# A state space mixer's output matmuls: the two halves of the groups in turn, state terms ahead of the local term

## The chip, the cores and the metric

The kernel runs on one core of one Trainium2 chip. Its time is the device time of one execution in microseconds (us). The kernel before ran three times, and one more execution was recorded by the hardware profiler. The engines are TensorE (PE, with its weight loads as PEld), VectorE (DVE), ScalarE (ACT), GpSimd (POOL) and SyncE (SP), which issues DMAs.

## The reference, cut to what matters

The network has four layers over 512 tokens of width 1024. The change lies in the mixer of the first one, a diagonal complex state space model with 64 groups of 16 channels and 64 states each:

```python
bu_re = jnp.einsum('bsgc,gpc->bsgp', u, bb_re)
bu_im = jnp.einsum('bsgc,gpc->bsgp', u, bb_im)
_, _, h_re, h_im = lax.associative_scan(
    _complex_linear_combine, (a_re_t, a_im_t, bu_re, bu_im), axis=1)
y = (jnp.einsum('bsgp,gcp->bsgc', h_re, c_re.astype(f32))
     - jnp.einsum('bsgp,gcp->bsgc', h_im, c_im.astype(f32)))
y = y + d_skip.astype(f32).reshape(N_GROUPS, SSM_GROUP) * u
y = jax.nn.gelu(y.reshape(bsz, seq, D_MODEL)).astype(x.dtype)
val, gate = jnp.split(y @ w_glu, 2, axis=-1)
return (val * jax.nn.sigmoid(gate)) @ w_out
```

After it come a layer norm, a feed-forward layer, an attention layer with its own feed-forward layer, and two more layers of another kind.

## The kernel before, in words

The mixer (`s5`) cuts the 512 tokens into 64 chunks of 8. Within a chunk the output is a sum of two terms. The local term is the chunk's own input times a block Toeplitz matrix `T` (contraction over all 128 partitions, 8 tokens by 16 channels). The state term is the state at the chunk's start, `H`, times an output matrix `ca`, with a real and an imaginary part (`r` = 0, 1; contraction over 64 states).

The 64 groups are taken as two halves `h` of 32. The half `h` = 0 has its states on partitions 0 to 63, and its 64 chunks fill output partitions 0 to 63; the half `h` = 1 has the other 64 of both. The 32 groups of a half are taken in four rounds `q` of eight (`j`). For each round there are these steps:

- `state_in(q)` builds input matrices with PE (L692) and multiplies the input by them (L700), into two PSUM banks `e`. L700 takes `h` = 0 and `h` = 1 in turn.
- `states(q)` scans the 64 chunks on DVE (L109, L724) and leaves `H`. The scan's input and `H` are tiles with the tag `gi`, which has three buffers.
- `outmat(q)` computes `ca` on DVE. For rounds 0 and 1 it lies in the memory that the GLU's input `yl` takes over later (tag `xl`).
- `local(q)` computes the Toeplitz matrix's coefficients with PE (L760, in four strips of 32 columns), adds the skip term on DVE (`ks`, L119) and writes them to DRAM (`kd`, L766). `toeplitz(q)` reads them back as `T` with eight DMAs (L775). There are two `T` buffers.
- `outputs(q)` multiplies both terms into four PSUM banks, one for each `h` and each `jj` (four of the eight `j`), and applies the GELU (L793, ACT). L789 is the local term, L791 the state term. An fp32 matmul stands in the trace as two records.
- `place(q)` transposes the result on PE (L127) and splits it into a rounded part and a rest (`xh` on ACT, `xl` on DVE).

`head_a`, `head_b` and `head_c` are the first matmuls of the GLU behind it (L265 to L267), interleaved with the last rounds. The steps are called in the order 'outputs(0), states(2), outmat(3), local(2), toeplitz(2), outputs(1), place(0), local(3), toeplitz(3), states(3), place(1), outputs(2), place(2), head_a, outputs(3), head_b, place(3), head_c'. A planner then orders the instructions of each engine: it simulates the program and takes, among the instructions that are ready, the one that stands first in the program. Each engine works through its list in that order. Two matmuls that write the same PSUM bank keep their order.

Of the kernel before, what the change touches and what calls it, by code (L numbers as in the profile page):

```python
# [16 lines left out]
P = 128  # L17
# [49 lines left out]
class Net:  # L67
# [428 lines left out]
    def s5(self, x, lam_re, lam_im, log_dt, b_re, b_im, c_re, c_im, d_skip, early=None, w_glu=None):  # L496
        nc = self.nc
# [5 lines left out]
        with self.tc.tile_pool(name="s5b", bufs=1, side="right", reuse_waits="tile") as pb, \  # L503
# [11 lines left out]
            if early:  # L515
                p, w = early
# [127 lines left out]
            for r in range(2):  # L644
                G.memset(bz[r], 0.0)
                for h in range(2):
                    sl = slice(h * 64, h * 64 + 64)
# [6 lines left out]
            u = self.tile(pb, [P, 32, P], F32, "u")  # L654
# [124 lines left out]
            def outputs(q):  # L779
                ca, H, T = (st[q][k] for k in ("ca", "H", "T"))  # L780
                yg = st[q]["yg"] = self.tile(pb, [P, 8, 8, 16], F32, "yg", 2)
                for jj in range(2):
                    pss = [self.bank(), self.bank()]
                    for h in range(2):
                        sl = slice(h * 64, h * 64 + 64)
                        for m in range(4):
                            j = jj * 4 + m
                            o = pss[h][sl, m * P:(m + 1) * P]
                            nc.tensor.matmul(o, u[:, q * 8 + j, sl], T[:, m * 2 + h, jj], start=True, stop=False)  # L789
                            for r in range(2):  # L790
                                nc.tensor.matmul(o, H[sl, r, j], ca[sl, r, j].rearrange("p d c -> p (d c)"),  # L791
                                                 start=False, stop=r == 1)
                        nc.scalar.activation(yg[sl, :, jj * 4:jj * 4 + 4].rearrange("p t j c -> p j t c"),  # L793
                                             pss[h][sl].rearrange("p (j t c) -> p j t c", j=4, t=8),
                                             AF.Gelu_apprx_tanh)
# [68 lines left out]
            state_in(3)  # L864
            head_load(0)
            outputs(0)
            states(2)
            outmat(3, V)
            local(2)
            toeplitz(2)  # L870
            outputs(1)
            yh, yl = self.fm_x()
            place(0)
            local(3)
            toeplitz(3)
            states(3)
            place(1)
            outputs(2)
            place(2)
            head_a(0)  # L880
# [905 lines left out]
```

## Time and profile before

| | |
|---|---|
| median of three runs | 2530.16 us (2527.28 to 2530.75) |
| profiled execution | 2529.88 us, span 2528.1 us |
| mean granted TensorE clock | 0.973 of full speed |
| PE busy | 2411.3 us, 95% |
| DVE, ACT, POOL busy | 1559.1, 968.8, 389.0 us |

The span runs from the first to the last instruction. Records name the line of the kernel, the output and inputs by the program's names (buffer numbers left out), and the shape. In a timeline the first column is the start, the second the length of the merged piece, and in brackets stands the idle time of the engine before it and what ended it. A PE record lasts until its result is out, so records overlap: the rate is read from starts. The granted clock is given as a share of 2.4 GHz.

### The profile page before, as it was taken

The numbers are of one execution on the slowest core, as the hardware profiler recorded it, in microseconds if no ns is written. First come the engines' busy times: TensorE is split into PE (matmuls) and PEld (weight loads), VectorE is DVE, ScalarE is ACT, GpSimd is POOL, SyncE is SP. The second block draws the span as 40 slices with busy tenths as digits, with TensorE's granted clock in tenths as the row PEclk, the third lists the DMA queues.
The fourth block names the chain that finished last, engine by engine and source line by source line (L and its number), as shares of the span: only waits on it lengthen the run. The fifth ranks groups of instructions, "written<-read, shape, count | busy, mean of one in ns | idle before, by whom it ended". The sixth has DMA issues, their size and how long they took to land.

```text
span 2528.1 us, 30717 instructions
## 1 busy us (share of the span) xinstructions
PE 2411.3 (95%) x11961; PEld 1988.5 (79%) x11961; DVE 1559.1 (62%) x2898; ACT 968.8 (38%) x1563; POOL 389.0 (15%) x378
## 2 busy tenths in 40 slices
PE   7799999999989999999999999999989998999997
PEld 6667888888877888888776878888877687888886
DVE  8744366765666567765695573555569556355655
ACT  4213235445245335444246432333324643223331
POOL 1100110000231220000246220000034622000001
PEclk9779999999999999999999999999999999999999
DMA  4224243322221533222232235232123123423211
GB/s 110 57 57 133 84 150 101 98 88 81 85 71 51 167 92 109 92 92 67 78 127 51 84 121 179 67 133 67 60 86 127 51 86 107 167 67 117 84 59 59
DMA packets 182897, 237.55 MB, mean 94 GB/s; under 512 B 19728, under 2 KB 118816, under 8 KB 182688
## 3 DMA queue, kind: packets, MB, share of 16 engines
q1 hardware_dynamic: 182752, 235.59, 29.5%
q8 instruction: 94, 1.54, 0.3%
q14 instruction: 51, 0.42, 0.1%
HBM read 224.56 MB, written 11.01 MB: 93 GB/s over the span
## 4 chain that ended last, share of the span: by engine, by line
PE 82%; DVE 15%; ACT 2%; DMA 1%; issue 1%; SPq 0%; DVEq 0%; POOL 0%; ACTq 0%
PE ps L265 26%; PE ps L266 25%; PE ps L267 25%; PE ps L127 3%; DVE x L119 2%; PE ps L791 2%; DVE sc L1451 2%; DVE m L1450 2%; DVE x L109 1%; PE ps L789 1%; PE ps L459 1%; DVE vy L109 1%; DVE xl L109 1%; DVE ab L109 1%; DVE sc L119 1%
## 5 line engine op out<-in xcount | busy, mean ns | idle before, releaser
L109 POOL TENSOR_TENSOR wl<-wr,wh 128x1024 fp32r<-128x1024 f32 (+4 forms) x124 | 278.2, 2253 | 1810.9 <-ACT wh L249 1127.0
L249 ACT CAST wh<-wr 128x1024 fp32r<-128x1024 f32 (+4 forms) x300 | 305.7, 1021 | 578.8 <-PE ps L266 287.4
L267 PE MATMUL ps<-xh,wl 128*128 128x512 f32 x1248 | 485.9, 390 | 4.3 <-DVE wl L109 4.3
L265 PE MATMUL ps<-xh,wh 128*128 128x512 f32 x1248 | 486.2, 390 | 0.0
L266 PE MATMUL ps<-xl,wh 128*128 128x512 f32 x1248 | 486.2, 390 | 0.0
L109 DVE TENSOR_TENSOR wl<-wr,wh 128x1024 fp32r<-128x1024 f32 x176 | 217.2, 1236 | 226.5 <-ACT wh L249 225.4
L109 DVE TENSOR_TENSOR wl<-wq,wh 128x1024 fp32r<-128x1024 f32 x140 | 170.5, 1221 | 178.1 <-ACT wh L249 177.7
L267 PEld LDWEIGHTS ps<-xh,wl 128*128 128x128 f32 x1248 | 234.7, 188 | 53.4 <-DVE wl L109 4.7
L265 PE MATMUL ps<-wh,xh 128*128 128x512 f32 (+4 forms) x704 | 270.9, 386 | 4.5 <-DVE rp L109 2.0
L266 PEld LDWEIGHTS ps<-xl,wh 128*128 128x128 f32 x1248 | 234.8, 188 | 48.8
L265 PEld LDWEIGHTS ps<-xh,wh 128*128 128x128 f32 x1248 | 234.6, 188 | 48.6
L266 PE MATMUL ps<-wl,xh 128*128 128x512 f32 (+4 forms) x704 | 263.6, 375 | 0.0
L267 PE MATMUL ps<-wh,xl 128*128 128x512 f32 (+4 forms) x704 | 262.6, 376 | 0.5 <-DVE xl L109 0.5
L249 ACT CAST wh<-wq 128x1024 fp32r<-128x1024 f32 x140 | 147.3, 1052 | 284.1 <-PE ps L266 234.5
L266 PE MATMUL ps<-wl,sh 128*128 128x512 f32 x560 | 217.8, 389 | 0.0
L267 PE MATMUL ps<-wh,sl 128*128 128x512 f32 x560 | 217.5, 389 | 0.0
L265 PE MATMUL ps<-wh,sh 128*128 128x512 f32 x560 | 216.9, 389 | 0.0
L265 PEld LDWEIGHTS ps<-wh,xh 128*128 128x128 f32 x704 | 136.9, 195 | 31.4 <-ACT xh L122 3.5
L267 PEld LDWEIGHTS ps<-wh,xl 128*128 128x128 f32 x704 | 136.1, 194 | 22.1 <-DVE xl L109 1.1
L266 PEld LDWEIGHTS ps<-wl,xh 128*128 128x128 f32 x704 | 137.0, 195 | 18.5
L109 DVE TENSOR_TENSOR x<-x,ps 128x512 f32<-128x512 f32 x156 | 103.0, 681 | 73.4 <-PE ps L267 73.1
L127 PE MATMUL ps<-ident,x 128*128 128x128 f32 x576 | 97.6, 289 | 47.3 <-DVE x L119 30.8
(368 smaller groups left out, 3910.8 us busy)
## 6 DMA issues: line engine op xcount, KB each, us to landing
wr<-in_w_ffn_in_dram SPq DMA_DIRECT2D x44, 1024.0 KB, 5.1
wr<-in_w_ff_dram SPq DMA_DIRECT2D x40, 1024.0 KB, 5.5
wq<-in_w_ff_dram SPq DMA_DIRECT2D x24, 1024.0 KB, 5.1
wq<-in_w_ffn_out_dram SPq DMA_DIRECT2D x16, 1024.0 KB, 8.2
wr<-in_w_in_dram SPq DMA_DIRECT2D x12, 1024.0 KB, 5.5
wr<-in_w_ple_gate_dram SPq DMA_DIRECT2D x8, 1024.0 KB, 5.1
wr<-in_ssm_w_glu_dram SPq DMA_DIRECT2D x6, 1024.0 KB, 5.6
xs<-x SPq DMA_DIRECT2D x24, 256.0 KB, 2.0
```

What stands on the lines that cost most here:

```text
L109: (eng or self.nc.vector).tensor_tensor(out, a, b, op)
L119: (eng or self.nc.vector).scalar_tensor_tensor(out, a, s, b, op0, op1)
L127: self.nc.tensor.transpose(out, in_, self.ident[:k, :k])
L249: self.nc.scalar.copy(hi, src)
L265: mm(ps, lh, rh, start=first, stop=False)
L266: mm(ps, lh, rl, start=False, stop=False)
L267: mm(ps, ll, rh, start=False, stop=last)
L459: self.nc.tensor.matmul(bk[:, c], w[:, kt], self.Xh(kt)[:, c], start=kt == 0 and w is hi, stop=False)
L789: nc.tensor.matmul(o, u[:, q * 8 + j, sl], T[:, m * 2 + h, jj], start=True, stop=False)
L791: nc.tensor.matmul(o, H[sl, r, j], ca[sl, r, j].rearrange("p d c -> p (d c)"), start=False, stop=r == 1)
L1450: self.nc.vector.max(m8, s)
L1451: self.nc.vector.match_replace(s, m8, s, -3e38)
```

## The change

In `outputs`, the loop over the two halves goes inside the loop over `m`. For each `m` the four state matmuls come first: the real part of half 0 and half 1, then the imaginary part of half 0 and half 1. Then come the two local matmuls, half 0 and half 1. The first state matmul now clears the bank region (`start`), and the local one ends the accumulation (`stop`). The two GELUs come after all matmuls of a `jj`. Operands, banks and the number of instructions stay the same.

```diff
-                    for h in range(2):
-                        sl = slice(h * 64, h * 64 + 64)
-                        for m in range(4):
-                            j = jj * 4 + m
-                            o = pss[h][sl, m * P:(m + 1) * P]
-                            nc.tensor.matmul(o, u[:, q * 8 + j, sl], T[:, m * 2 + h, jj], start=True, stop=False)
-                            for r in range(2):
-                                nc.tensor.matmul(o, H[sl, r, j], ca[sl, r, j].rearrange("p d c -> p (d c)"),
-                                                 start=False, stop=r == 1)
+                    halves = [slice(h * 64, h * 64 + 64) for h in range(2)]
+                    for m in range(4):
+                        j = jj * 4 + m
+                        o = [pss[h][sl, m * P:(m + 1) * P] for h, sl in enumerate(halves)]
+                        for r in range(2):
+                            for h, sl in enumerate(halves):
+                                nc.tensor.matmul(o[h], H[sl, r, j], ca[sl, r, j].rearrange("p d c -> p (d c)"),
+                                                 start=r == 0, stop=False)
+                        for h, sl in enumerate(halves):
+                            nc.tensor.matmul(o[h], u[:, q * 8 + j, sl], T[:, m * 2 + h, jj], start=False, stop=True)
+                    for h, sl in enumerate(halves):
                         nc.scalar.activation(yg[sl, :, jj * 4:jj * 4 + 4].rearrange("p t j c -> p j t c"),
                                              pss[h][sl].rearrange("p (j t c) -> p j t c", j=4, t=8),
                                              AF.Gelu_apprx_tanh)
```

## Rows read from the trace of the kernel before

**Rows 1.** The page's table of engines: busy time, share, instructions.

```profile
PE 2411.3 (95%) x11961; PEld 1988.5 (79%) x11961; DVE 1559.1 (62%) x2898; ACT 968.8 (38%) x1563; POOL 389.0 (15%) x378
```

**Rows 2.** Stretches: length, busy PE, PEld, DVE, ACT, POOL, clock, DMA share, GB/s.

```profile
110.00:122.00 12.00, 12.00 (x47) 7.18 (x46) 0.28 (x1) 2.23 (x3) 2.34 (x1) 0.50 0.00 0
...
125.00:126.00 1.00, 1.00 (x8) 0.67 (x6) 1.00 (x3) 0.84 (x2) 0.00 (x0) 0.59 0.00 0
...
130.00:131.00 1.00, 0.52 (x6) 0.52 (x8) 1.00 (x3) 0.00 (x0) 0.00 (x0) 0.50 0.46 131
...
152.00:157.00 5.00, 5.00 (x46) 3.81 (x46) 5.00 (x12) 3.52 (x8) 0.00 (x0) 0.55 0.01 3
157.00:165.00 8.00, 8.00 (x53) 5.17 (x52) 1.71 (x5) 2.06 (x5) 0.00 (x0) 1.00 0.46 88
```

**Rows 3.** Timeline of PE, in rounds 0 and 2.

```profile
100.58 1.03 PE L791 MATMUL ps<-xl,gi 64*64 64x128 f32 x8 [2.17 <-DVE gi L109]
...
114.56 0.69 PE L789 MATMUL ps<-T,u 128*64 128x128 f32 x2
115.18 1.11 PE L791 MATMUL ps<-xl,gi 64*64 64x128 f32 x4
116.22 0.69 PE L789 MATMUL ps<-T,u 128*64 128x128 f32 x2
...
160.41 0.43 PE L789 MATMUL ps<-T,u 128*64 128x128 f32 x2
160.77 0.65 PE L791 MATMUL ps<-ca,gi 64*64 64x128 f32 x4
161.35 0.43 PE L789 MATMUL ps<-T,u 128*64 128x128 f32 x2
```

**Rows 4.** Timeline of PE, ahead of rounds 1 and 2.

```profile
124.74 1.27 PE L789 MATMUL ps<-T,u 128*64 128x128 f32 x8
...
130.48 1.54 PE L791 MATMUL ps<-xl,gi 64*64 64x128 f32 x10 [2.00 <-DVE gi L109]
131.95 0.69 PE L789 MATMUL ps<-T,u 128*64 128x128 f32 x2
...
154.80 1.92 PE L127 MATMUL ps<-ident,yg 128*128 128x128 f32 x8
```

**Rows 5.** Stretches with L700 alone, then L760: length, busy PE, PEld, clock, DMA.

```profile
48.20:50.28 2.08, 2.08 (x64) 1.95 (x64) 1.00 0.00 0
...
78.03:79.07 1.04, 1.04 (x30) 0.84 (x30) 1.00 0.00 0
```

**Rows 6.** Timeline of DVE, 109 to 152 us.

```profile
109.08 1.19 DVE L109 TENSOR_TENSOR ca<-pw,bt 128x1024 f32<-128x1024 f32 x1
122.97 0.68 DVE L109 TENSOR_TENSOR gi<-tab,ps 128x504 f32<-128x504 f32 x1 [12.69 <-PE ps L791]
...
129.75 1.28 DVE L109 TENSOR_TENSOR gi<-gi,rt 128x512 f32<-128x512 f32 x2
...
144.45 1.22 DVE L724 TENSOR_TENSOR_SCAN g<-ro,gi 128x512 f32<-128x512 f32 x1
151.97 0.42 DVE L109 TENSOR_TENSOR xl<-ps,xh 128x256 fp32r<-128x256 f32 x1 [6.30 <-PE ps L791]
```

**Rows 7.** Timeline of PE behind round 2 and at the mixer's end.

```profile
172.44 1.10 PE L127 MATMUL ps<-ident,yg 128*128 128x128 f32 x8 [0.68 <-ACT yg L793]
...
185.74 0.43 PE L789 MATMUL ps<-T,u 128*64 128x128 f32 x2
...
200.78 0.50 PE L265 MATMUL ps<-xh,gi 128*128 128x512 f32 x1
...
216.96 0.50 PE L267 MATMUL ps<-xh,wl 128*128 128x512 f32 x1 [4.26 <-DVE wl L109]
```

**Rows 8.** Timeline of SP's DMA issues.

```profile
159.69 4.82 SPq L775 DMA_DIRECT2D T<-kd  x8
164.56 1.21 SPq L242 DMA_DIRECT2D wr<-in_ssm_w_glu_dram  x2
```

## The prediction

> **What bounds the kernel now.** I read first the page's table of engines. The reader sees that TensorE (PE) is busy for 95% of the span [rows 1], so only time taken off PE's own row, or off a wait of PE, can show at the end. The changed lines run once, in the first 8% of the span. I therefore read the table of stretches for 97 to 215 us, with the granted clock. The reader sees PE busy all through 110 to 122 us while DVE has next to nothing to do, and the clock at 0.50 (1.2 GHz); it is at 1.00 (2.4 GHz) only from 157 us on [rows 2]. Third, PE's timeline, for the price of the changed lines. One (m, h) is six records, as each fp32 matmul stands there as two passes: two passes of the T term, then four of the state terms. At 1.2 GHz the T passes take 0.62 us and the state passes 1.04, together 1.66; at 2.4 GHz 0.36 and 0.58, together 0.94 [rows 3]. A group has 16 of these. Outputs(0) and outputs(1) run at the low level, outputs(2) and outputs(3) at the high one.
>
> **Part 1: alternating halves.** The two halves use different halves of the array's columns, and the state terms different halves of its rows too. The trace of before has both kinds of neighbours by accident, where the planner pulled the first matmul of each of the four banks ahead. Eight T passes start at 124.74 us and take 1.27 us, 0.16 us each, against 0.31 in line. Ten state passes start at 130.48 us and the next T at 131.95: 0.147 us each, against 0.26 in line [rows 3, 4]. The clock in those two stretches was 0.50 to 0.59 [rows 2]. Eight full-array transposes with the same 128 columns took 1.92 us at the low level, 0.24 each [rows 4]; a pass that costs less than that isn't alone in the array. L700, which alternates halves in two passes each, as the change will, runs 64 passes in 2.08 us, 0.033 each. L760, in four column strips, runs 30 passes of 128 columns in 1.04 us, 0.035 each, though four passes in a row go to one strip [rows 5]. So I take it that both kinds overlap in pairs. A pair (m, both halves) then costs what one (m, h) costs now: 1.66 or 0.94 us, with the switch between T and state terms in it. A group has 8 pairs: 13.3 us at 1.2 GHz, 7.5 us at 2.4.
>
> The bounds of this price: full overlap as above; none at all, when a pair costs two (m, h) less one of the two switches. A switch is 0.94 less six passes of 0.145, 0.07 us, and 0.10 at the low level. That is 1.81 us a pair and 14.5 a group at 2.4 GHz; 3.22 and 25.8 at 1.2. I take the full overlap, since the rows of this very line are nearest to it.
>
> **Part 2: state terms first.** Now T matmuls run while H is still being computed. They can't any more: within a bank each matmul follows the one before, and the first one now reads H. All of a group's work lies behind H. That is in the 13.3 us. What it takes away is a wait for T's DMA ahead of the state terms; T is now wanted a microsecond later, which is worth nothing, since PE waits for H there anyway [rows 3].
>
> **The sum along the chain.** Outputs(0) starts at 100.58 us, when DVE has H ready, and holds the `gi` buffer that DVE writes at 122.97, after 12.69 us of idleness that PE's L791 ends [rows 3, 6]. So it takes 22.3 us of the path and will take 13.3: it ends at 113.9, gain 9.0. DVE's list before that is done at 110.3, and so isn't in the way [rows 6].
>
> From there DVE needs 7.5 us (122.97 to PE's start at 130.48 [rows 4, 6]) for H of group 1. This stays, and outputs(1) starts at 121.5. It lasts 21.4 us now (130.48 to the DVE write that waits for it, 151.97, less 0.1) and 13.3 then: it ends at 134.8, gain 8.1, in all 17.1.
>
> DVE is the next to be late. It has 15.2 us of work behind the start of outputs(1) (to 145.67) and then idles 6.30 [rows 6]. Moved with outputs(1) it is done at 136.7, 1.9 us after PE. PE meanwhile has the transposes of place(0) and place(1) and local(3), 4.8 us that end now at 156.7 [rows 4], so DVE's lag is covered; uncovered it would cost up to 1.9.
>
> Outputs(2) at 2.4 GHz: 15.0 to 7.5, gain 7.5. The two activations of the last bank pair now come both at the end. PE waits 0.68 us for the last one before place(2) [rows 7]; one more costs 0.6. At outputs(1) the transposes of place(0) cover this, at outputs(3) the 4 us of head_b.
>
> Outputs(3), 185.74 to 200.78 [rows 7]: gain 7.5. Its T comes by DMA. The eight transfers are issued in the 4.8 us from 159.69, behind local(3) and DVE's `ks`, and ahead of the first GLU weights at 164.56 [rows 8]. They move with DVE, by 15.3, so the last is issued by 149.2. Outputs(3) will start at 185.74 less 24.0, 161.7. This leaves 12 us for the landing.
>
> Behind the mixer the 4.26 us that PE waits for `wl` at 216.96 [rows 7], and what follows, hang on the end of the mixer's last matmuls and on buffers that it gives free; they move as a block. From there PE is nearly always busy, so what is gained stays.
>
> Sum: 9.0 + 8.1 + 7.5 + 7.5 - 0.6 = 31.5 us. The profiled execution took 2529.88 us, 0.28 less than the median of the runs; 2529.9 - 31.5 = 2498.4, and I say 2498.5.
>
> **Rivals.** *Faster still: the clock rises in the first two groups.* It rose by 126 us, after local(2) and the T matmuls that ran ahead, and by 157, after local(3) and transposes; it didn't in 110 to 122, when PE did only unpaired work on a part of the array [rows 2]. Whether paired work raises it, no row shows. If it rises early in both groups, outputs(0) takes 7.5 us, but DVE is done only at 110.3: gain 12.6. Outputs(1) runs from 117.9 to 125.4. PE's sum is 12.6 + 13.9 + 7.5 + 7.5 - 0.6 = 40.9; DVE is then 8 us behind PE with 4.8 of cover, so I take some 38: 2492, at the lowest 2489.
>
> *Half the overlap: order.* If a pass must wait for the one before it in its own tile, and holds the other half's passes behind it, two and two in turn give five steps for eight state passes and three for four T passes. A pair then costs 5 x 0.145 + 3 x 0.18 = 1.27 us, a group 10.1; at 1.2 GHz 5 x 0.26 + 3 x 0.31 = 2.23 and 17.8. Gain 4.5 + 3.6 + 4.9 + 4.9 - 0.6 = 17.3: 2512.6. L760's 0.035 us in fours speaks against it. The Trainium skill, page "TensorE: Matmul & The Clock Gate", section "Part 3: Packing small matmuls — row/col tiling", speaks for it: by that section matmuls start and end in strict program order, and weight loads overlap running matmuls only where the row groups differ. The rate of L700, whose two halves share all rows, doesn't bear out the second half of that.
>
> *Only T overlaps.* The state terms differ in rows as well as columns, and the one row for them is the stretch of ten. A pair is then 2.70 us at 1.2 GHz and 1.52 at 2.4, a group 21.6 and 12.2. Gain 0.7 - 0.2 + 2.9 + 2.9 - 0.6 = 5.7: 2524.
>
> *Slower: no overlap, and T no longer runs ahead.* With the upper bound of the price, outputs(0) takes 25.8 us for 22.3 and outputs(1) 25.8 for 21.4, as the work done while H was awaited now lies behind it. The other two gain 0.5 each, the activation costs 0.6: 7.5 us slower, 2537.4. It decides when alternating saves under a fifth of what full overlap does (7.5 of 39 us). Against it stand the rows of part 1.
>
> **How the numbers follow.** About 0.2%, 5 us, is what a measurement of this kernel can tell from no change. Full overlap at the low clock in the first two groups 0.50; with a rising clock 0.24; half the overlap 0.12; only T 0.05; none 0.07; 0.02 that the planner orders something else worse and eats the gain. The first three are faster: 0.86, with half of the fourth 0.88. Same 0.05, slower 0.07. The range from 2488 to 2514 holds the first three.
>
> **What would show it.** Right: L791 starting in runs of eight passes 0.07 us apart at 2.4 GHz (0.13 at 1.2), T in runs of four; outputs(2) and outputs(3) in 7.5 us each; DVE's idleness of 12.69 us shrunk to about 4, that of 6.30 gone; the mixer's last matmul near 181 us instead of 212. Granted clocks of 1.00 ahead of outputs(2) show the faster rival, groups of 10 and 18 us the half overlap, 14 to 15 us at 2.4 GHz and no T ahead of H the slower one. The prediction is wrong also if DVE's lag grows into a wait of outputs(2), or if the order behind the mixer differs.

## The result, and the profile after

The changed kernel takes 2495.41 us (median of four runs, 2494.14 to 2495.57), the kernel before 2530.32 (four runs, the three shown and one more). The ratio is 0.9862, with a 95% interval of 0.9849 to 0.9875: 34.9 us faster, where 31.7 were forecast for the likeliest case. The profiled execution took 2495.57 us, with a span of 2493.8.

The page's table of engines, of the kernel after; [rows 1] answers to it:

```profile
PE 2373.8 (95%) x11961; PEld 1965.3 (79%) x11961; DVE 1560.8 (63%) x2898; ACT 968.7 (39%) x1563; POOL 389.0 (16%) x378
```

PE has the same number of instructions and is busy for 37.5 us less; the other engines are within 2 us of before. So time was taken off PE's own row, where it sets the end.

The timeline of PE after, in outputs(0), outputs(1), and outputs(3) (the first column is the start):

```profile
99.03 1.51 PE L790 MATMUL ps<-xl,gi 64*64 64x128 f32 x10 [3.66 <-DVE gi L109]
...
101.09 1.12 PE L790 MATMUL ps<-xl,gi 64*64 64x128 f32 x8
102.14 0.69 PE L793 MATMUL ps<-T,u 128*64 128x128 f32 x4
102.76 1.12 PE L790 MATMUL ps<-xl,gi 64*64 64x128 f32 x8
...
106.53 0.65 PE L790 MATMUL ps<-xl,gi 64*64 64x128 f32 x4
107.11 0.43 PE L793 MATMUL ps<-T,u 128*64 128x128 f32 x2
...
118.61 1.12 PE L790 MATMUL ps<-xl,gi 64*64 64x128 f32 x8 [6.23 <-DVE gi L109]
...
158.43 0.65 PE L790 MATMUL ps<-ca,gi 64*64 64x128 f32 x8
159.01 0.44 PE L793 MATMUL ps<-T,u 128*64 128x128 f32 x4
159.38 0.65 PE L790 MATMUL ps<-ca,gi 64*64 64x128 f32 x8
```

The state terms are L790 now and the local terms L793; a record is one pass. From the starts: at 1.2 GHz eight state passes take 1.05 us (101.09 to 102.14) and four T passes 0.62, so a pair takes 1.67; at 2.4 GHz 0.58 and 0.37 (158.43, 159.01, 159.38), so 0.95. [rows 3] has the same times for half as many passes. The two halves overlap fully: the single records at 158.43 us start in twos, 0.006 us apart, with 0.109 us from one two to the next (0.160 behind the first), and passes of one half alone keep the same steps before (from 187.05 us on). From 105.8 to 109.9 us, in the second `jj` of outputs(0), the planner has set the halves apart, and passes stand in fours and twos as before (106.53, 107.11): some 2 us of this group's gain are missing there.

Stretches after, with the columns of [rows 2]:

```profile
102.00:106.00 4.00, 4.00 (x32) 2.41 (x30) 4.00 (x5) 0.09 (x1) 0.00 (x0) 0.58 1.16 263
106.00:110.00 4.00, 4.00 (x32) 2.46 (x32) 2.63 (x3) 2.14 (x3) 1.74 (x1) 1.00 0.59 62
118.00:122.00 4.00, 3.39 (x22) 2.10 (x22) 4.00 (x5) 0.37 (x1) 2.10 (x1) 0.50 0.35 97
122.00:126.00 4.00, 4.00 (x50) 2.63 (x50) 3.96 (x6) 1.23 (x3) 0.15 (x2) 0.95 0.39 85
126.00:132.00 6.00, 5.62 (x86) 3.99 (x84) 6.00 (x10) 3.07 (x5) 0.00 (x0) 1.00 0.04 6
...
136.00:140.00 4.00, 1.50 (x16) 1.16 (x18) 3.82 (x11) 1.94 (x7) 0.00 (x0) 0.93 0.00 0
140.00:145.00 5.00, 3.84 (x34) 2.11 (x30) 0.76 (x2) 2.52 (x6) 1.37 (x1) 0.71 0.38 92
...
158.00:166.00 8.00, 8.00 (x99) 4.96 (x97) 0.00 (x0) 1.18 (x2) 0.00 (x0) 1.00 0.01 2
```

The clock now rises inside outputs(0) and again inside outputs(1), after some 6 and 4 us of paired matmuls; in [rows 2] it was at 0.50 through 12 us of unpaired ones. It falls again between 139 and 140 us, behind a hole in PE's work: 1.50 us busy in 136 to 140.

DVE's timeline after, and the chain of waits from 130 to 145 us (start, length, what):

```profile
111.01 0.68 DVE L109 TENSOR_TENSOR gi<-tab,ps 128x504 f32<-128x504 f32 x1 [2.37 <-PE ps L790]
...
177.11 0.33 DVE L119 SCALAR_TENSOR_TENSOR a<-a,ang 128x160 f32<-128x160 f32 x1 [3.62 <-PE ps L267]
```

```profile
130.66 1.22 DVE g L724
132.49 1.24 DVE g L724
133.75 0.69 DVE gi L109
136.58 1.20 DVE gi L109 x2
137.78 0.68 DVE xl L109 x2
138.50 0.65 PE ps L790 x6
139.52 1.05 PE ps L790 x8
```

The 12.69 us of DVE's idleness [rows 6] have become 2.37, and the 6.30 behind outputs(1) are gone. In their place the chain goes through DVE, where that of before stayed on PE: the scans of round 3, then the `xl` of place(1), and only then PE. The last line of DVE's two is the first work behind the mixer (`a`, which waits for head_c); it began at 211.84 us before and begins at 177.11 now.

The account by stages, in us, each from one start to the next:

| stage | before | after | gain | forecast |
|---|---|---|---|---|
| start of the span to outputs(0) | 100.58 | 99.03 | 1.55 | 0 |
| outputs(0), to the DVE write that waits for it | 22.39 | 11.98 | 10.41 | 9.0 |
| DVE's H of group 1 | 7.51 | 7.60 | -0.09 | 0 |
| outputs(1) | 21.39 | 10.00 | 11.39 | 8.1 |
| transposes, local(3), to outputs(2) | 4.78 | 3.10 | 1.68 | 0 |
| outputs(2), to the transposes of place(2) | 15.79 | 13.42 | 2.37 | 6.9 |
| place(2), head_a, to outputs(3) | 13.30 | 13.30 | 0 | 0 |
| outputs(3), head_b, place(3), head_c | 26.10 | 18.68 | 7.42 | 7.5 |
| all behind | 2316.26 | 2316.69 | -0.43 | 0 |
| sum | | | 34.3 | 31.5 |

34.3 us is also the difference of the spans. In the table, outputs(2) holds the one big miss and outputs(0) and outputs(1) the gains beyond the forecast.

### The profile page after: what moved, and what is told of

It reads as the page before. It is cut to its first block, busy times and chain, and to the rows that moved or that the text cites. A ratio compares the mean times of both kernels' runs of the same rounds, so it can differ in the third digit from the quotient of the medians.

```text
span 2493.8 us, 30715 instructions
## 1 busy us (share of the span) xinstructions
PE 2373.8 (95%) x11961; PEld 1965.3 (79%) x11961; DVE 1560.8 (63%) x2898; ACT 968.7 (39%) x1563; POOL 389.0 (16%) x378
## 4 chain that ended last, share of the span: by engine, by line
PE 83%; DVE 14%; ACT 2%; issue 1%; DMA 0%; SPq 0%; DVEq 0%; POOL 0%; ACTq 0%
PE ps L265 26%; PE ps L266 25%; PE ps L267 25%; PE ps L127 3%; DVE x L119 2%; DVE sc L1453 2%; DVE m L1452 2%; DVE x L109 1%; PE ps L459 1%; PE ps L790 1%; DVE vy L109 1%; DVE sc L119 1%; DVE xl L109 1%; PE ps L692 1%; DVE st L360 1%
```

## The experiments

Four questions: what each part of the edit is worth alone (e1, e2); whether the order of the passes limits the overlap (e3, e6b); where outputs(2)'s missing gain went (e4, e5); and whether outputs(0) and outputs(1) are held by DVE (e7, e8). The diffs are against the changed kernel. In the table the mixer is the time from the first state matmul of outputs(0) to `a` behind head_c, the rest is the span less the start of `a`. Both come from the one profiled execution of each kernel. Ratios are to the kernel before in runs on the same chip.

| kernel | median us | ratio (95%) | mixer | rest |
|---|---|---|---|---|
| before | 2530.3 | 1 | 111.26 | 2316.3 |
| after | 2495.41 | 0.9862 (0.9849 to 0.9875) | 78.08 | 2316.7 |
| e1_state_first | 2536.9 | 1.0025 (1.0014 to 1.0036) | 120.87 | 2317.1 |
| e2_alternate_T_first | 2494.52 | 0.986 (0.9844 to 0.9875) | 77.82 | 2311.7 |
| e3_fours | 2496.62 | 0.9868 (0.9853 to 0.9883) | 77.76 | 2317.9 |
| e4_one_bank | 2492.97 | 0.985 (0.9831 to 0.9869) | 73.81 | 2318.5 |
| e5_place1_later | 2502.79 | 0.9898 (0.9884 to 0.9913) | 73.52 | 2326.5 |
| e6b_sixteens | 2513.68 | 0.9947 (0.993 to 0.9964) | 83.54 | 2326.3 |
| e7_load_later | 2507.97 | 0.992 (0.9905 to 0.9935) | 74.48 | 2330.4 |
| e8_one_bank_load_later | 2491.83 | 0.9856 (0.9841 to 0.987) | 73.31 | 2320.3 |

**e1_state_first: the order of the terms alone.** The halves stay one behind the other, the state terms come first. (Only added lines are shown.)

```diff
+                    for h in range(2):
+                        sl = slice(h * 64, h * 64 + 64)
+                        for m in range(4):
...
+                            for r in range(2):
+                                nc.tensor.matmul(o, H[sl, r, j], ca[sl, r, j].rearrange("p d c -> p (d c)"),
                                                  start=r == 0, stop=False)
...
+                            nc.tensor.matmul(o, u[:, q * 8 + j, sl], T[:, m * 2 + h, jj], start=False, stop=True)
```

> State terms ahead of the local term as in the change, but the halves one after the other as in the kernel before. If the gain comes from the two halves sharing the array, nothing is gained here, and the T matmuls that ran ahead of H are lost: 3 to 8 us slower than before, about 2533 to 2538, the clock at 1.2 GHz all through outputs(0) and outputs(1), four state passes in 1.04 us there. If the gain came from moving the local term behind the state terms (fewer waits for T's DMA), this is as fast as the changed kernel, about 2495.

It took 2536.9 us, against 2529.75 for the kernel before on the same chip. PE's and DVE's timelines of e1, and two of its stretches:

```profile
98.85 1.51 PE L790 MATMUL ps<-xl,gi 64*64 64x128 f32 x8 [3.68 <-DVE gi L109]
...
100.91 1.11 PE L790 MATMUL ps<-xl,gi 64*64 64x128 f32 x4
101.95 0.69 PE L792 MATMUL ps<-T,u 128*64 128x128 f32 x2
102.56 1.11 PE L790 MATMUL ps<-xl,gi 64*64 64x128 f32 x4
```

```profile
124.44 0.68 DVE L109 TENSOR_TENSOR gi<-tab,ps 128x504 f32<-128x504 f32 x1 [15.99 <-PE ps L790]
```

```profile
106.00:110.00 4.00, 4.00 (x15) 2.35 (x16) 2.45 (x3) 0.58 (x1) 0.00 (x0) 0.50 0.35 39
...
140.00:150.00 10.00, 10.00 (x37) 5.70 (x37) 9.93 (x16) 1.18 (x2) 0.00 (x0) 0.50 0.00 1
```

The reader sees the price of unpaired passes: 1.65 us for one (m, h), 25.6 us for outputs(0) (98.85 to 124.44), and 7.2 us more in all. So the order of the terms brings none of the gain; with e2, below, all of it comes with the alternation. The slower rival had 25.8 and 7.5 us, but for another order, with the halves in turn; that these figures are near is chance (see e6b). Nor does e1 show that the overlap is the whole of the gain: alternating also halves the number of changes between state and local matmuls, and e1 keeps all of them. The clock stays at 0.50 through both groups, with the same work ahead of them as in after, where it rose in both.

**e2_alternate_T_first: the alternation alone.**

```diff
+                        for h, sl in enumerate(halves):
+                            nc.tensor.matmul(o[h], u[:, q * 8 + j, sl], T[:, m * 2 + h, jj], start=True, stop=False)
                         for r in range(2):
                             for h, sl in enumerate(halves):
                                 nc.tensor.matmul(o[h], H[sl, r, j], ca[sl, r, j].rearrange("p d c -> p (d c)"),
-                                                 start=r == 0, stop=False)
-                        for h, sl in enumerate(halves):
-                            nc.tensor.matmul(o[h], u[:, q * 8 + j, sl], T[:, m * 2 + h, jj], start=False, stop=True)
+                                                 start=False, stop=r == 1)
```

> Halves alternate as in the change, but the local term stays ahead of the state terms. If alternating is the whole gain, this is the changed kernel's time within 3 us, 2492 to 2498, perhaps a little less, since three T matmuls run ahead of H before outputs(0) and four before outputs(1). If the order of the terms mattered, it stays near 2525 to 2530.

2494.52 us. The mixer is 0.3 us shorter than after's, which is nothing here; outputs(0) starts 3.2 us later (102.23) and the rest is 5.0 us shorter, and these two cancel in part in the total. T does run ahead of H again, as PE's timeline shows ahead of outputs(1):

```profile
114.44 1.14 PE L789 MATMUL ps<-T,u 128*64 128x128 f32 x8
```

The eight T passes take 1.14 us at a granted clock of 1.00; the 1.27 us of [rows 4] were at 0.50 to 0.59, so the two can't be compared as rates. With the alternation the order of the terms is worth nothing that can be measured.

**e3_fours: four state passes of one half, then four of the other.**

```diff
-                        for r in range(2):
-                            for h, sl in enumerate(halves):
+                        for h, sl in enumerate(halves):
+                            for r in range(2):
```

> The changed kernel with the state terms in fours: both parts of half 0, then both of half 1, then the local terms in turn. If each half's part of the array takes its own passes as they come, fours overlap as twos do: eight state passes still in 0.58 us at 2.4 GHz, total 2494 to 2497. If a pass that waits holds the other half's behind it, eight state passes take seven steps, 1.02 us: 3.5 us more in each group, 2509 to 2515.

2496.62 us, within 1.2 of after. PE's timeline of e3 in outputs(2):

```profile
132.37 0.66 PE L790 MATMUL ps<-ca,gi 64*64 64x128 f32 x8
132.96 0.44 PE L793 MATMUL ps<-T,u 128*64 128x128 f32 x4
133.33 0.66 PE L790 MATMUL ps<-ca,gi 64*64 64x128 f32 x8
```

Eight state passes still take 0.59 us. If a pass that waits for its own tile held back those behind it, fours would need seven steps, by the prediction's price 1.02 us. In the single records the second half's first pass starts at 132.385, 0.013 us behind the first half's first (132.372), and the first half's second only at 132.532, although three passes of the first half stand ahead of the second half in the program. So that rival falls, in the trace of after already and here more plainly. The Trainium skill, page "TensorE: Matmul & The Clock Gate", section "Part 3: Packing small matmuls — row/col tiling", has matmuls start and end in strict program order; this trace doesn't bear that out for the starts of two diagonal tiles.

**e6b_sixteens: how far the overlap reaches.** Sixteen state passes of half 0, sixteen of half 1, then eight and eight T passes. Only the first matmul of a bank clears it, and the accumulation ends with the last; the sums are the same. (Only added lines are shown; `mm` is the matmul call, `ms` the four `m`.)

```diff
+                    for h, sl in enumerate(halves):
+                        for m in ms:
+                            for r in range(2):
+                                mm(o[h][m], H[sl, r, jj * 4 + m], ca[sl, r, jj * 4 + m].rearrange("p d c -> p (d c)"),
+                                   start=r == 0 and m == 0, stop=False)
+                    for h, sl in enumerate(halves):
+                        for m in ms:
+                            mm(o[h][m], u[:, q * 8 + jj * 4 + m, sl], T[:, m * 2 + h, jj], start=False, stop=m == 3)
```

> The changed kernel with all 16 state passes of half 0 of a jj, then the 16 of half 1, then 8 local passes of each half. If the array takes each half's passes from as far behind as 16 passes, the 32 state passes still take about 2.3 us at 2.4 GHz and outputs(3) 7.2 to 7.6 us: 2493 to 2497 in all. If it only looks a few passes ahead, the halves run mostly one after the other: 32 state passes in 3.5 to 4.6 us, outputs(3) in 11 to 14 us, 2510 to 2530 in all, as in the kernel before, where T stood between the halves' state passes.

2513.68 us. The profiled execution is 14.8 us longer than after's: 5.5 us lie in the mixer, and 9.6 in the rest, in a layer that the edit doesn't touch (see e5). Without those 9.6 the total would stand below the range that was expected for halves one behind the other, so the total decides nothing, and the stage has to. PE's timeline of e6b in outputs(3), at a granted clock of 1.00:

```profile
161.72 3.32 PE L791 MATMUL ps<-ca,gi 64*64 64x128 f32 x32
164.98 1.58 PE L795 MATMUL ps<-T,u 128*64 128x128 f32 x16
166.49 3.32 PE L791 MATMUL ps<-ca,gi 64*64 64x128 f32 x32
```

The 32 state passes take 3.26 us, the sixteen T passes 1.51, and outputs(3) 9.53 (161.72 to 171.25), for 7.63 in after (158.43 to 166.06) and 15.04 before. The starts of the trace's single records, to 0.001 us, say why. Passes of one tile start 0.109 us apart, the second 0.160 behind the first; from the last pass of a kind to the first of the other kind (state or T) it is 0.20. The records don't name the half, but two series with this step stand out, sixteen passes each:

| half, pass | start, us |
|---|---|
| first half, 12th to 16th | 162.974, 163.083, 163.192, 163.301, 163.410 |
| second half, 1st to 4th | 163.089, 163.249, 163.358, 163.467 |

The second half's first pass starts 0.006 us behind the 13th of the first half, when three of that half are still to start. T does the same: the second half's first pass starts at 165.469, behind the fifth of eight at 165.464, again with three to come. So it is in outputs(0) too, at 1.2 GHz (101.758 behind 101.752), and in outputs(2). In e3's fours three passes are all that stand between. So TensorE took up the other tile's work past three waiting passes, and in sixteens or eights not past more. An estimate from these steps: 32 state passes would take 1.9 us fully overlapped and 3.7 one half behind the other, sixteen T passes 1.0 and 1.9; e6b has a quarter of the overlap in the first and a little under half in the second.

That outputs(3) is still 5.5 us shorter than before has another reason. A change of kind costs 0.20 us and a slower first step, some 0.14 us more than two steps within a kind. Before there were two changes for each (m, h), after the edit there are two for each pair, in e6b two for each `jj`. An estimate of after's order with no overlap at all, at 2.4 GHz: (0.160 + 6 x 0.109 + 0.20) + (0.160 + 2 x 0.109 + 0.20) = 1.59 us for a pair. Two (m, h) took 1.88 before, and the pair takes 0.95. So of the 0.93 us saved, some 0.3 would come with the fewer changes alone, and some 0.64 come from the overlap. No run has after's order without the overlap, so this division stays an estimate.

The clock rose in e6b too, some 10.5 us into outputs(0) and as late into outputs(1), though most passes ran alone:

```profile
104.00:109.00 5.00, 5.00 (x27) 4.34 (x26) 4.35 (x4) 1.72 (x3) 0.00 (x0) 0.50 0.89 88
109.00:113.00 4.00, 4.00 (x42) 3.66 (x41) 1.40 (x2) 0.90 (x2) 2.44 (x3) 0.97 0.01 1
```

**e4_one_bank: both halves in one PSUM bank, one GELU for both.** If outputs(2) waits for a bank that DVE's `xl` holds, two banks fewer for a group should end the wait.

```diff
-                    pss = [self.bank(), self.bank()]
+                    ps = self.bank()
...
-                        o = [pss[h][sl, m * P:(m + 1) * P] for h, sl in enumerate(halves)]
+                        o = [ps[sl, m * P:(m + 1) * P] for sl in halves]
...
-                    for h, sl in enumerate(halves):
-                        nc.scalar.activation(yg[sl, :, jj * 4:jj * 4 + 4].rearrange("p t j c -> p j t c"),
-                                             pss[h][sl].rearrange("p (j t c) -> p j t c", j=4, t=8),
-                                             AF.Gelu_apprx_tanh)
+                    nc.scalar.activation(yg[:, :, jj * 4:jj * 4 + 4].rearrange("p t j c -> p j t c"),
+                                         ps.rearrange("p (j t c) -> p j t c", j=4, t=8),
+                                         AF.Gelu_apprx_tanh)
```

> The changed kernel with both halves of a jj in one PSUM bank (each on its own 64 partitions) and one GELU of 128 partitions in place of two of 64. If halves overlap whatever bank they write, the wait of 2.55 us of outputs(2) for a bank goes, with the low clock behind it, and outputs(0) is paired to its end: 2487 to 2492. If two halves of the rows can't write one bank at once, the state terms are in line again: 1.16 in place of 0.58 us for eight passes at 2.4 GHz, 5 us more in each group, up to 8 at 1.2 GHz: 2515 to 2525.

2492.97 us, a little above the 2487 to 2492 expected. The place in question, PE's timeline after and then that of e4:

```profile
135.52 0.43 PE L790 MATMUL ps<-ca,gi 64*64 64x128 f32 x2
138.50 0.65 PE L790 MATMUL ps<-ca,gi 64*64 64x128 f32 x6 [2.55 <-DVE xl L109]
139.08 0.44 PE L793 MATMUL ps<-T,u 128*64 128x128 f32 x4
139.45 1.12 PE L790 MATMUL ps<-ca,gi 64*64 64x128 f32 x8
...
145.13 1.09 PE L127 MATMUL ps<-ident,yg 128*128 128x128 f32 x8 [1.29 <-ACT yg L795]
```

```profile
131.48 0.65 PE L790 MATMUL ps<-ca,gi 64*64 64x128 f32 x8
...
138.15 0.65 PE L790 MATMUL ps<-ca,gi 64*64 64x128 f32 x8
138.74 0.44 PE L793 MATMUL ps<-T,u 128*64 128x128 f32 x4
140.49 1.09 PE L127 MATMUL ps<-ident,yg 128*128 128x128 f32 x8 [1.31 <-ACT yg L794]
```

In e4 outputs(2) runs from 131.48 to 139.11 without a hole, 7.6 us as forecast for 2.4 GHz, and place(2) starts 9.01 us behind its start instead of 13.42. The 4.4 us between are the wait for the bank, 2.55, and the low clock behind it, 1.9 by difference. The mixer is 4.3 us shorter, the time only 2.4, with overlapping intervals: 1.8 went to the rest.

outputs(0) ran in whole pairs in e4, from 98.67 to 108.3, 9.7 us, but outputs(1) started 19.15 us behind outputs(0), against 19.58 in after: DVE had no hole there and came to its write at 110.33 (that of after waited to 111.01). So here DVE's list held the first group, as the faster rival had it; a `ca` of 3.33 us just ahead, 1.20 in after, is part of it.

**e5_place1_later: the same wait, taken away by order.** place(1) is called behind outputs(2), so its `xl` no longer stands between outputs(2) and its banks.

```diff
-            place(1)
             outputs(2)
+            place(1)
             place(2)
```

> The changed kernel with place(1) called behind outputs(2), so that outputs(2) finds its PSUM banks free. If the 2.55 us that outputs(2) waits there for a bank, and the low clock in the 4 us behind it, are what keeps round 2 from its 7.5 us, then outputs(2) takes 7.6 us and the time falls by 3 to 5 us, to 2491. If DVE's list is the limit there in any order, round 2 is as late as before, and the time stays within 1.5 us of 2495.4 or rises, as place(1) then stands behind outputs(2) on PE.

2502.79 us. The mixer did what was expected: outputs(2) takes 7.6 us, with no wait, and the mixer 73.52. But the total, expected near 2491, rose: 10 us came back behind the mixer, nearly all in the last of the four layers, some 1.7 ms later. PE's timeline of e5 there, and that of after at its like:

```profile
1887.79 0.69 PE L127 MATMUL ps<-ident,x 128*128 128x128 f32 x2 [6.65 <-ACT x L1491]
```

```profile
1886.76 0.44 PE L127 MATMUL ps<-ident,x 128*128 128x128 f32 x2 [1.16 <-ACT x L1491]
```

PE runs out of other work there and waits 6.65 us for ACT, and the granted clock is 0.91 in 1846 to 1900 us and 0.86 in 1950 to 2000 (0.97 and 1.00 in after). The instructions of PE and ACT stand in another order in that layer than in after, though no line of it was touched: the planner simulates the whole program, and its choices differ from there on. e6b and e7 have the same wait with 8.18 us. Why the planner's order came out worse in these three and not in e2, e3, e4, e8 isn't settled.

**e7_load_later and e8_one_bank_load_later: what holds DVE ahead of outputs(0).** (The diff is e7's; e8 has that of e4 besides.) In after, DVE's `ks` takes 4.62 us just ahead of H, while POOL splits the GLU's first weights. `head_load` is the call that loads them; it is moved from ahead of outputs(0) to ahead of place(1). e8 adds the one bank.

```diff
             state_in(3)
-            head_load(0)
             outputs(0)
...
             states(3)
+            head_load(0)
             place(1)
```

> The changed kernel with the GLU's first weight pieces (head_load) called ahead of place(1) in place of ahead of outputs(0). In the changed kernel two small DVE operations on ks take 4.6 us there, while GpSimd splits the weight pieces, and H of round 0 stands behind them on DVE. If the two engines hold each other up, H of round 0 comes 3 to 4 us earlier without this, and the time falls by as much, to 2491 to 2493. If the 4.6 us have another cause, they stay, and so does the time, within 1.5 us.

> One PSUM bank for both halves, and head_load later as well. If the two act in different places they add up: 2.5 us from the bank and 3 to 4 from GpSimd, 2489 to 2490. If DVE's list bounds the mixer in both, no more than the better of the two alone, 2492 to 2493.

DVE's timeline and POOL's in after, and then DVE's in e7:

```profile
93.65 4.62 DVE L119 SCALAR_TENSOR_TENSOR ks<-dm,dk,ks 128x16 f32<-128x16 f32 x2
```

```profile
92.79 5.46 POOL L109 TENSOR_TENSOR ab<-bm,ab 128x1024 fp32r<-128x1024 f32 x2 [8.95 <-ACT ab L822]
```

```profile
96.61 2.82 DVE L109 TENSOR_TENSOR gi<-gi,rt 128x512 f32<-128x512 f32 x1
99.36 0.22 DVE L119 SCALAR_TENSOR_TENSOR ks<-dm,dk,ks 128x16 f32<-128x16 f32 x1
```

The edit didn't take the work beside DVE away: in e7 POOL still splits `ab` from 93.25 us on, for 5.64 us. `ks` went to 0.22 us each, but outputs(0) started no earlier (99.58): DVE's list was ordered anew, and now it is a `gi` of H that stands beside POOL's work and takes 2.82 us. So neither of the two outcomes expected came. outputs(1) began at 114.92, 15.3 us behind outputs(0). e7's mixer is 3.6 us shorter than after's, and the time 12.6 longer; most of that lies in the last layer, where the wait of 8.18 us came with it. In e8 it didn't come: 2491.83 us, the shortest median of all, mixer 73.31, with a wait for T's DMA of 1.47 us in outputs(2) that after doesn't have. That is between the two outcomes expected for e8. e4 and e8 are 2.4 and 3.6 us below after, but their intervals overlap with after's, so they are not told apart from it.

## Why the prediction was right, and where its terms were not

- **Full overlap of both kinds**: shown. A pair costs 1.67 and 0.95 us where 1.66 and 0.94 were taken, and in the single records both halves keep the step that one half has alone. Only-T and half-the-overlap fall with it. That the state terms overlap too could only be read off one stretch of ten records ahead of the change [rows 4]; it held.
- **The price without overlap**: mis-sized, which the forecast of the likeliest case didn't need. The prediction took 0.145 us for an unpaired state pass and 0.07 for a change of kind. 0.145 is (0.160 + 2 x 0.109 + 0.20) / 4, with the change in it; the step is 0.109, and a change costs some 0.14 more. So no overlap is, by estimate, 1.59 us a pair and 12.7 a group at 2.4 GHz, not 1.81 and 14.5, and by the steps at 1.2 GHz (0.27 first, 0.213, 0.35 at a change) 2.94 and 23.5, not 3.22 and 25.8. By these figures the slower rival would have come out near the time of before (1.2 + 2.1 - 2.3 - 2.3 + 0.6 us, two groups slower and two faster), not 7.5 us above it. And not all of the gain is the overlap's: at 2.4 GHz some 0.3 of the 0.93 us of a pair would come from fewer changes of kind.
- **The clock in the first two groups**: mis-sized, by 1.4 + 3.3 us. The forecast kept it low through outputs(0) and outputs(1), and the rival had it high from the start. It lay between: the first 6 us of outputs(0) and the first 4 of outputs(1) ran at 1.2 GHz, the rest at 2.4. The sign that the prediction named for the faster rival, a clock of 1.00 ahead of outputs(2), came true. Where I had written that no row shows whether paired work raises it, after against e1 shows that the edit does; pairing isn't the only thing that can, as e6b shows, where it rose later and most passes ran alone. The transposes and local(3) behind outputs(1) gained 1.7 us that way as well, for which the forecast had nothing.
- **DVE's lag behind outputs(1), "covered"**: this step failed. The rising clock shortened both outputs(1) and its cover (4.78 to 3.10 us), and the lag, priced at 1.9 uncovered, became the chain's own: scans, `xl`, then PE, with a wait of 2.55 us inside outputs(2) and 1.9 of low clock behind it. outputs(2) gained 2.4 us instead of 6.9. The prediction named this as one of the things that would make it wrong; e4 shows the place and the size by taking it away.
- **outputs(3) and the extra activation**: 7.42 us for 7.5. The wait for ACT ahead of place(2) grew from 0.68 [rows 7] to 1.29 us, by the 0.6 that was priced. One GELU for both halves (e4) leaves it at 1.31, so the wait isn't that one instruction's: in e4 ACT's last two GELUs stand behind its six `xh` of place(1).
- **T no longer ahead, worth nothing**: shown by e2 against after (0.9 us, T first the faster, inside the intervals; 0.3 us in the mixer). Without the alternation it is worth 7 us (e1).
- **T's DMA and the work behind the mixer**: in after no wait for T appeared; PE's 4.26 us for `wl` stand behind the mixer as before [rows 7], now at 182.24; the rest is 0.4 us longer. The earlier start of outputs(0), 1.55 us, isn't shown to be a gain of the change: DVE is 1.6 us earlier already at the `gi` that starts at 89.98 us before and at 88.34 after, ahead of any changed line, and in kernels with the same work ahead outputs(0) starts anywhere from 98.67 to 102.23.
- **The planner**: 0.02 was little for it. In three of the seven edits that kept the overlap in whole or in part, the order of the last layer came out some 10 us worse (the rest 2326.3 to 2330.4 us, for 2316.7). That the change didn't meet this is not something the prediction's rows could tell.

So the errors in size cancel in part: 1.4 + 3.3 + 1.7 more from the clock, 4.5 less from DVE, and 1.55 from the start. The mechanism, two halves that overlap fully, was right; that the total came within 3.1 us is partly luck, as the clock of the likeliest case didn't come and DVE took back most of what the rising clock gave.

## What to carry to other kernels

Small fp32 matmuls that use different parts of the array should stand in turn in the program, here at most four passes of one part in a row, and matmuls of one kind should stand together, since each change of kind had its price. Look in the trace for places where two of them came to be neighbours by accident, for they give the price; and read it from the starts of single records, since the average of a short group has the change of kind in it. When a stage on the path gets shorter, ask of the next engine's lag not only whether the cover hides it today, but whether the cover shrinks with the change too. And where a planner orders the whole program, compare the time behind the edited stage as a number by itself: here it moved by -5 to +14 us through edits that didn't touch it.

## What the hardware showed that was not expected

- The overlap of two diagonal 64x64 tiles is full when their passes stand in twos or fours (0.58 and 0.59 us for eight passes). In sixteens, and for the 128x64 tiles of T in eights, the second tile's first pass started when three of the first tile's were still to start (163.089 behind 163.083, 165.469 behind 165.464 in e6b).
- A change between 64x64 and 128x64 matmuls took 0.20 us from start to start at 2.4 GHz and 0.35 at 1.2, where passes of one tile follow each other in 0.109 and 0.213.
- The two halves, in different rows and columns of the array, can fill the same PSUM bank (other partitions of it) at the same rate: 0.59 us for eight passes in e4 (138.15 to 138.74), 0.58 in two banks. The Trainium skill, page "TensorEngine Tiling (Array Packing)", section "Gotcha 1: PSUM Pressure", says that different row tiles can't access one bank at the same time. These two tiles differ in their columns too, and e4's rate shows no loss.
- Some of DVE's work stretches beside POOL's: two `ks` of 16 columns took 4.62 us together while POOL worked from 92.79 to 98.25, and 0.22 each outside of that (e7), where a `gi` of 512 columns took 2.82 instead of 0.68. The Trainium skill, page "GPSIMD Engine Reference", section "1. Specifications", names this contention, for DVE instructions with two SBUF inputs; both of these have them. Not all such work stretches: in e7 a `ca` with two inputs, which starts at 100.85 just behind a POOL piece of 3.47 us at 100.79, took its usual 1.21.
